# The indexer's low-part product over 128 rows, and two gate projections moved from the index loop to the threshold search

## The chip, the core and the metric

The kernel runs on one core of a Trainium2 chip. The core has a matrix engine (TensorE, PE in the profile), three engines for elementwise work (VectorE or DVE, ScalarE or ACT, GpSimd or POOL), and queues of transfers, here all issued by SyncE (SP). The engines run their own instruction lists in order and wait for one another at semaphores. The metric is the device time of one execution in microseconds; the time before is the median of three.

## What is computed

A trunk of two layers over 1024 tokens of 1024 channels, each with a mixer, a cross-attention of four heads into 256 memory tokens, a SiLU gate over all 2048 branch channels, an output projection and a layer norm. Layer A mixes by a depthwise convolution. Layer B, around which the change lies, is sparse attention: an indexer with 8 heads of 64 channels scores all keys for a query, the 256 best admissible keys are kept, and 12 attention heads work on those.

```python
iscore = relu(einsum('bqhd,bsd->bqhs', qib, k_idx))
iscore = einsum('bqh,bqhs->bqs', wb, iscore)
iscore = where(admiss, iscore, NEG)
_, sel = top_k(iscore, 256)
...                      # softmax attention over the selected keys, ALiBi distances
y = concatenate([y_mix, y_mem]) * silu(gate)
x = layer_norm(ALPHA * x + y @ w_out)
```

## The kernel before

All products run on TensorE in a float32 format of reduced width, so each operand is held as a high and a low part (`split_w`, `split_ps`), and a projection is three products per 128-row block: high by high (L149), high weight by low input (L151), low weight by high input (L153). `project_steps` gives them one at a time. A gate projection (`gate_steps`) is 128 gate columns for 1024 tokens: 2 halves of 512 columns, 8 blocks, 3 products, so 48 products of 512 columns, two silus on ScalarE (L706) and a store. Its weights come as two pieces of 256 KB through the SP queue (L122) into three raw buffers; ScalarE copies out the high part (L131), or GpSimd does (L129) where `pool_only` is set, and GpSimd subtracts for the low part (L132). High and low parts have six buffers, which is three gates.

The order in layer B is: projections for the indexer; the index loop; the threshold search and selection; attention.

The index loop goes over six query blocks (7, 6, 2, 5, 4, 3; block b has 128(b+1) keys) and in each over 8 index heads. Keys are cut into one or two parts of at most 512. For each part two products go into one PSUM bank. The stationary tile `t` has the 64 high-part channels of the head's queries in one half of its rows (`a`) and the 64 low-part channels in the other; `khh` holds the high part of the keys in both halves and `kll` their low part in both. So the first product (L777, all 128 rows) gives high times high plus low times high, and the second (L778, the 64 rows of `a`) adds high times low. ScalarE then takes the relu (L783; two PSUM tiles and two relu tiles) and VectorE multiplies by the head's weight and adds to the block's scores `xs` (L786, L788). After each head's last product, `FILL[b]` products of the first `FREE_GATES` gates are put into TensorE's list: 136 of 144 between the heads, and the rest behind the loop. There are 48 heads and 80 pairs of score products.

The threshold search finds the 256th largest score of each query bit by bit (31 rounds), with three blocks counted on VectorE (L829) and three on ScalarE (L835). The selection turns the scores into distances with a large one for what isn't selected (L896 to L905). Both have a low priority. The gates that are left, 12 of them, are put on TensorE behind the last score product, with `pool_only` weights, and after them the queries of the first two attention heads (`head_q`: 48 products each, and per half a copy on ScalarE, L806, and a subtraction on VectorE, L807). Attention scores (L951 to L953), their row maxima (L956) and the rest follow.

The order of instructions on each engine is made by a planner that simulates the engines, with the priorities above and `issue_after` edges; only what is quoted fixes a place by hand.

Of the kernel before, what the change touches and what calls it, by code (L numbers as in the profile page):

```python
# [18 lines left out]
PSUM = bass.MemoryType.PSUM  # L19

P = 128
T = 1024
# [31 lines left out]
FREE_GATES = 3  # L54
POOL_W = True
SELECT = (7, 4, 3, 6, 5, 2)
FILL = {7: 4, 6: 3, 5: 3, 4: 3, 3: 2, 2: 2}
# [7 lines left out]
def trunk(ctx, tc, x, mem, mem_g, mem_b, a_w_in, conv_w, conv_b, ln_g, ln_b,  # L65
          a_w_mkv, a_w_out, a_pg, a_pb, b_w_in, b_w_mkv, b_w_out, b_pg, b_pb, out, dbg=None):
    nc = tc.nc
# [13 lines left out]
    # ---------------------------------------------------------------- constants  # L81
# [7 lines left out]
    # per-channel vectors, channel on the partition: taps, conv bias, LN gain, LN bias, mem gain, mem bias  # L89
# [12 lines left out]
    # PSUM banks: projections ("pj") and the rest ("pt"), from the pools of the phase  # L102
# [14 lines left out]
    # ---------------------------------------------------------------- helpers  # L117
    def split_w(src3, shape, place=None, pool_only=False):
        """Loads a [128, 512]-word piece of a weight and splits it into two float32r parts."""
        n = uid()  # L120
        raw = wp.tile(shape, F32, tag="wraw", bufs=3, name=f"wr{n}")
        nc.sync.dma_start(raw, src3)  # L122
        if place is None:
            hi = wp.tile(shape, F32R, tag="whi", bufs=6, name=f"wh{n}")
            lo = wp.tile(shape, F32R, tag="wlo", bufs=6, name=f"wl{n}")
        else:
            hi, lo = place(n)
        if pool_only:
            nc.gpsimd.tensor_copy(hi, raw)  # L129
        else:  # L130
            nc.scalar.activation(hi, raw, AF.Copy)  # L131
        nc.gpsimd.tensor_tensor(lo, raw, hi.bitcast(F32), op=OP.subtract)  # L132
        return hi, lo

    def load_cols(w, c0, n=P, pool_only=False):
        """Columns c0:c0+n of a [1024, C] weight as two pieces of four 128-row blocks."""
        res = []
        for g in range(2):
            res.append(split_w(w[g * 512:(g + 1) * 512, c0:c0 + n].rearrange("(k p) c -> p k c", p=P), [P, 4, n],
                               pool_only=pool_only))  # L140
        return res

    def project_steps(pieces, mhi, mlo, c0, n, o):
        """o[cols, n] = W^T X over the moving operand's columns c0:c0+n, one product at a time."""
        for k in range(KD):
            hi, lo = pieces[k // 4]
            wh, wl = hi[:, k % 4, :], lo[:, k % 4, :]
            xh, xl = mhi[:, k, c0:c0 + n], mlo[:, k, c0:c0 + n]
            nc.tensor.matmul(o, wh, xh, start=(k == 0), stop=False)  # L149
            yield  # L150
            nc.tensor.matmul(o, wh, xl, start=False, stop=False)  # L151
            yield
            nc.tensor.matmul(o, wl, xh, start=False, stop=(k == KD - 1))  # L153
            yield

    def run(steps):
        """All that is left of some steps, and what they return."""
        while True:
            try:
                next(steps)  # L160
            except StopIteration as end:
                return end.value
# [12 lines left out]
    def ln_moments(src):  # L175
        """Mean and 1/sqrt(var + eps) of [128, 1024] along the free axis."""
        n = uid()
        st = small.tile([P, 2, 6], F32, tag="bnst", name=f"bnst{n}")
        for i in range(2):
            nc.vector.bn_stats(st[:, i, :], src[:, i * 512:(i + 1) * 512])  # L180
        mv = small.tile([P, 2], F32, tag="bnmv", name=f"bnmv{n}")
        nc.vector.bn_aggr(mv, st)
        rs = small.tile([P, 1], F32, tag="bnrs", name=f"bnrs{n}")
        nc.scalar.activation(rs, mv[:, 1:2], AF.Sqrt, bias=eps)
        nc.vector.reciprocal(rs, rs)
        return mv[:, 0:1], rs

    def ln_stats(src):
        """Scale and bias that normalize."""
        mean, rs = ln_moments(src)  # L190
        nb = small.tile([P, 1], F32, tag="bnnb", name=f"bnnb{uid()}")
        nc.vector.tensor_scalar(nb, mean, rs, -1.0, op0=OP.mult, op1=OP.mult)
        return rs, nb
# [7 lines left out]
    def layer_norm_late(dst, src, g, b, o):  # L201
        """The same in fewer steps, written out by halves."""
# [7 lines left out]
    def transpose_in(src, hi, lo, t, f=None):  # L210
        """[128 tok, 1024] -> columns t*128.. of the transposed hi and lo operands."""
# [11 lines left out]
    # ================================================================ layer A  # L223
    SC = {}
    with ExitStack() as actx:
# [14 lines left out]
        # ---- x and the vectors  # L240
# [29 lines left out]
        # ---- memory tokens: LN, transposed  # L270
# [23 lines left out]
        def mem_k(w, h, kv=None, raw=None):  # L294
            """K^T of one head of the memory attention, into kv = [K hi | V hi | K lo | V lo] or raw = [K | V]."""
# [8 lines left out]
        def mem_v(w, h, kv=None, raw=None):  # L304
            """V of one head, likewise."""
# [13 lines left out]
        def silu_gate(pl, w, c0, dst):  # L319
            """silu of 128 gate columns, transposed, into dst [128, 1024]."""  # L320
            pc = load_cols(w, c0)
            for hf in range(2):
                o = psum()
                project(pc, xhi, xlo, hf * 512, 512, o)
                nc.scalar.activation(dst[:, hf * 512:(hf + 1) * 512], o, AF.Silu)

        def mem_q(pl, tags, pc):
            """Queries of one head, transposed, in two parts; the products one at a time."""
# [9 lines left out]
        def mem_scores(pl, tags, q, kv, hf, banks_s):  # L338
            """Softmax over the memory tokens for half of the queries."""
# [26 lines left out]
        def mem_values(pl, tags, pn, kv, hf, sg, y, bank_pv, between=lambda ins: None):  # L366
            """Probabilities, transposed, times values, gated: half of y [128, 1024]."""
# [19 lines left out]
        # ---- gated conv input and the convolution  # L387
# [30 lines left out]
        def conv_pair(hs, i0):  # L418
            """Depthwise causal convolution of two channel tiles, taps interleaved."""
# [17 lines left out]
        def conv_stat(i):  # L437
            """Running sums over channels of the convolution less the mean of its first 128 channels."""
# [78 lines left out]
        # ---- conv LN statistics per token, then broadcast to all channels  # L517
# [22 lines left out]
        def load_y(pl, tag, src, dh, dl, gate=None, sub=None):  # L540
            """A branch in two parts, times silu(gate) where that is still to be done."""
# [23 lines left out]
        # ---- output projection of layer A  # L565
# [5 lines left out]
        def out_group(w_out, k0, yh, yl, acc, t_order, first=False, after=None, resident=None):  # L571
            """acc[tok, :] += y[:, 4 channel blocks] W_out[4 row blocks, :]."""
# [70 lines left out]
        def keep_a(hf, k):  # L643
            """Places for the last group's weights, all of which stay: four pieces where others are too."""
# [15 lines left out]
    # ================================================================ layer B  # L660
    with ExitStack() as bctx:
# [7 lines left out]
        def parts(b):  # L669
            """Key columns of a query block, cut into equal pieces of at most 512."""  # L670
# [28 lines left out]
        def gate_steps(pl, i, pool_only=False):  # L699
            """silu of 128 gate columns, transposed, into DRAM, one product at a time."""  # L700
# [10 lines left out]
        # ---- indexer  # L711
        with ExitStack() as ictx:
# [56 lines left out]
            for b in (7, 6, 2, 5, 4, 3):  # L769
# [3 lines left out]
                for h in range(IDX_HEADS):  # L773
                    t, a = qs[h]
                    S = psum_s()
                    for i, (c, m) in enumerate(pt):
                        nc.tensor.matmul(S[:, i, :m], t[:, blk], khh[:, c:c + m], start=True, stop=False)  # L777
                        step = nc.tensor.matmul(S[:, i, :m], t[a, blk], kll[a, c:c + m], start=False, stop=True)  # L778
# [18 lines left out]
        def head_q(h, pc):  # L797
            """Queries of a head, scaled by scale / slope; the products one at a time."""
# [11 lines left out]
        with ExitStack() as kctx:  # L810
            bm = kctx.enter_context(pool("bm"))

            # ---- exact 256th largest score of every query, bit by bit of its order-preserving key: state is the
            # float whose key has the bits found so far, and flipping a bit of it raises it (the lower bits of a
            # negative float count down). One group of blocks is counted on the vector engine (scores >= candidate),
            # the other on the scalar engine (scaled by 2^24, signs of candidate - score): there a candidate that is
            # itself a score may be refused, so the state may end one float low, which an exact count settles.
            def threshold():
# [44 lines left out]
                # scalar engine's group: drop what is too small to be a score, try the next float  # L863
# [13 lines left out]
            # ---- distances, with a large one where a key isn't selected (ties: lowest index first)  # L877
            def select():
# [7 lines left out]
                for b in SELECT:  # L886
# [12 lines left out]
                    # as many equal ones are taken as those above leave room for  # L899
# [20 lines left out]
        # ---- sparse attention: logits over slope in PSUM, one (head, two query blocks) step after the other  # L920
        with ExitStack() as tctx:
# [15 lines left out]
            def scores(h, j):  # L937
                """Softmax of query blocks 2j and 2j + 1."""
# [28 lines left out]
            def values(h, j, pt):  # L967
                """Transposed probabilities times values, gated."""
# [22 lines left out]
                for k in range(2 * j + 1):  # L991
                    nc.tensor.matmul(po, vh[:, k, :], ph[:, k, :], start=(k == 0), stop=False)
                    nc.tensor.matmul(po, vh[:, k, :], pl[:, k, :], start=False, stop=False)  # L993
                    if k == 2 * j:
                        # the last keys: for the second block only
# [40 lines left out]
            # one head after the other, scores a step ahead of values; between the products of a head run those of the  # L1036
            # next head's queries (of the last head: a gate that is left)
# [19 lines left out]
            def filler(i):  # L1057
                """Weights and steps of what runs beside head i of the sequence."""
# [19 lines left out]
            # places in the pool: what is written first lies clear of the selection's tiles  # L1078
# [22 lines left out]
    # ---- output projection of layer B  # L1101
# [66 lines left out]
```

## Time and profile before

| | us |
|---|---|
| median of 3 runs (lowest, highest) | 1740.03 (1739.72, 1742.56) |
| span of the profiled execution | 1739.0 |
| TensorE busy | 1677.7 |
| VectorE busy | 1171.7 |
| ScalarE busy | 756.5 |
| GpSimd busy | 688.5 |
| index loop, first to last of the main run of score products | 874.5 to 966.6 |
| threshold search and selection on VectorE | 968.2 to 1145.5 |

The profiled execution's own time is its span; no other time of it is listed, and the median of the runs is about one microsecond above it. A busy engine in this table is one that has an instruction in it. Products are pipelined, so the lengths of two that follow each other overlap, and what a product costs is the distance from its start to the next start.

### The profile page before, as it was taken

To read this page: it belongs to the slowest core of one execution; us is meant where nothing else is said; L and a number is where in the kernel's file an instruction comes from. 1 tells how busy PE (TensorE), PEld (TensorE's weight loads), DVE (VectorE), ACT (ScalarE), POOL (GpSimd) and SP (SyncE) were. 2 spreads that over 40 slices of the span, in tenths; PEclk is the share of its full clock that TensorE was granted. 3 is DMA by queue.
4 is the path that set the end of the run, shared out by engine and by line. 5 is a ranking of instruction groups with operands and counts; after the bars stand their busy time and mean duration, and the time that the engine had idled before them with its cause. 6 is when DMAs were issued, how large, how long until landed. Compare 5 with 4: busy or idle time off the path is not lost.

```text
span 1739.0 us, 22460 instructions
## 1 busy us (share of the span) xinstructions
PE 1677.7 (96%) x8214; PEld 1385.0 (80%) x8214; DVE 1171.7 (67%) x1800; ACT 756.5 (43%) x1416; POOL 688.5 (40%) x587
## 2 busy tenths in 40 slices
PE   7999999999999998999999999879999999999997
PEld 6877888888888876887855777668898988888886
DVE  3799999999995659256154899975545655535337
ACT  3333444443433514134453678455544544542121
POOL 2344554555546337334311333343223333343233
PEclk9999999999999998999999999989999999999999
DMA  5121222212233475122320233212112121137212
GB/s 180 49 61 61 85 61 73 82 63 90 69 110 122 146 278 169 61 80 88 93 56 25 74 91 90 75 37 80 62 55 73 61 80 49 61 120 266 93 43 97
DMA packets 138941, 156.88 MB, mean 90 GB/s; under 512 B 8074, under 2 KB 108426, under 8 KB 138832
## 3 DMA queue, kind: packets, MB, share of 16 engines
q1 hardware_dynamic: 138832, 155.47, 27.6%
q8 instruction: 64, 1.05, 0.2%
q14 instruction: 45, 0.37, 0.1%
HBM read 114.81 MB, written 38.80 MB: 88 GB/s over the span
## 4 chain that ended last, share of the span: by engine, by line
PE 62%; DVE 11%; ACT 3%; issue 2%; DMA 1%; POOL 1%; SPq 0%; DVEq 0%; ACTq 0%; POOLq 0%
PE pj L149 10%; PE pj L153 10%; PE pj L151 10%; PE pj L587 5%; PE pj L586 5%; PE pj L585 5%; DVE junk L829 3%; PE pt L981 2%; PE S L778 2%; PE S L951 1%; PE S L952 1%; PE S L953 1%; PE S L777 1%; PE pv L993 1%; PE pv L997 1%
## 5 line engine op out<-in xcount | busy, mean ns | idle before, releaser
L149 PE MATMUL pj<-xhi,wh 128*128 128x512 f32 (+2 forms) x1328 | 526.2, 396 | 17.6 <-DVE ql L807 3.6
L132 POOL TENSOR_TENSOR wl<-wr,wh 128x512 fp32r<-128x512 f32 (+1 forms) x260 | 350.8, 1355 | 460.6 <-ACT wh L131 444.9
L153 PE MATMUL pj<-xhi,wl 128*128 128x512 f32 (+2 forms) x1328 | 523.7, 394 | 0.0
L151 PE MATMUL pj<-xlo,wh 128*128 128x512 f32 (+2 forms) x1328 | 522.4, 393 | 0.6 <-DVE xlo L169 0.5
L433 DVE SCALAR_TENSOR_TENSOR acc<-h,chan,acc 128x996 f32<-128x996 f32 (+27 forms) x348 | 418.5, 1263 | 16.1 <-ACT acc L423 14.8
L149 PEld LDWEIGHTS pj<-xhi,wh 128*128 128x128 f32 (+1 forms) x1328 | 250.9, 189 | 73.8 <-DVE ql L807 6.9
L153 PEld LDWEIGHTS pj<-xhi,wl 128*128 128x128 f32 (+1 forms) x1328 | 250.9, 189 | 52.4 <-issue 3.7
L151 PEld LDWEIGHTS pj<-xlo,wh 128*128 128x128 f32 (+1 forms) x1328 | 251.1, 189 | 49.7 <-issue 2.0
L131 ACT ACTIVATE wh<-wr 128x512 fp32r<-128x512 f32 x236 | 147.2, 628 | 299.3 <-PE pj L151 155.4
L585 PE MATMUL pj<-wh,xhi 128*128 128x512 f32 x384 | 150.7, 399 | 9.3 <-DVE accA L592 5.6
L586 PE MATMUL pj<-wl,xhi 128*128 128x512 f32 x384 | 150.9, 395 | 0.0
L587 PE MATMUL pj<-wh,xlo 128*128 128x512 f32 x384 | 149.2, 394 | 0.0
L961 POOL TENSOR_SCALAR t<-t,smB 128x128 f32<-128x128 f32 (+3 forms) x96 | 71.6, 747 | 177.3 <-DVE smB L960 86.1
L956 DVE CUSTOM_DVE_ANT_0 t<-S,xs 128x128 f32<-128x128 f32 (+3 forms) x96 | 70.8, 755 | 64.9 <-PE S L953 42.9
L169 DVE TENSOR_TENSOR pl<-pt,ph 128x512 fp32r<-128x512 f32 (+1 forms) x120 | 69.2, 580 | 57.6 <-ACT ph L168 56.7
L585 PEld LDWEIGHTS pj<-wh,xhi 128*128 128x128 f32 x384 | 73.5, 191 | 27.6 <-DVE accA L592 6.4
L959 ACT ACTIVATE t<-t,mxB 128x128 f32<-128x128 f32 (+3 forms) x96 | 74.1, 774 | 49.0 <-DVE mxB L958 48.9
L168 ACT ACTIVATE ph<-pt 128x512 fp32r<-128x512 f32 (+1 forms) x120 | 60.2, 508 | 73.7 <-PE pt L981 67.7
L829 DVE TENSOR_SCALAR_CACHE_REDUCE junk<-xs,cand 128x1024 bf16<-128x1024 f32 (+2 forms) x93 | 89.9, 966 | 2.2
L835 ACT ACTIVATE junka<-xs,cand 128x896 bf16<-128x896 f32 (+2 forms) x93 | 80.3, 863 | 24.2 <-DVE cand L860 22.3
L587 PEld LDWEIGHTS pj<-wh,xlo 128*128 128x128 f32 x384 | 73.3, 191 | 16.0
L586 PEld LDWEIGHTS pj<-wl,xhi 128*128 128x128 f32 x384 | 73.4, 191 | 15.5
(273 smaller groups left out, 2726.4 us busy)
## 6 DMA issues: line engine op xcount, KB each, us to landing
wr<-in_a_w_in_dram SPq DMA_DIRECT2D x88, 256.0 KB
wr<-in_b_w_in_dram SPq DMA_DIRECT2D x76, 256.0 KB
wr<-in_a_w_out_dram SPq DMA_DIRECT2D x32, 256.0 KB
wr<-in_b_w_out_dram SPq DMA_DIRECT2D x32, 256.0 KB
yraw<-yb SPq DMA_DIRECT2D x16, 512.0 KB
gb<-gB SPq DMA_DIRECT2D x15, 512.0 KB
ga<-ga SPq DMA_DIRECT2D x12, 512.0 KB
gt<-ga SPq DMA_DIRECT2D x12, 512.0 KB
```

The lines of the kernel that those rows point to most:

```text
L131: nc.scalar.activation(hi, raw, AF.Copy)
L132: nc.gpsimd.tensor_tensor(lo, raw, hi.bitcast(F32), op=OP.subtract)
L149: nc.tensor.matmul(o, wh, xh, start=(k == 0), stop=False)
L151: nc.tensor.matmul(o, wh, xl, start=False, stop=False)
L153: nc.tensor.matmul(o, wl, xh, start=False, stop=(k == KD - 1))
L433: nc.vector.scalar_tensor_tensor(dst[:, s:], h[:, :T - s], w, acc[:, s:], op0=OP.mult, op1=OP.add)
L585: nc.tensor.matmul(o, yh[:, k, tsl], wh, start=(k == 0), stop=False)
L586: nc.tensor.matmul(o, yh[:, k, tsl], wl, start=False, stop=False)
L587: nc.tensor.matmul(o, yl[:, k, tsl], wh, start=False, stop=(k == 3))
L829: nc.vector.tensor_scalar(j[:, :nk(b)], xs(b), th[:, i:i + 1], None, op0=op, op1=OP.add, accum_out=c[:, i:i + 1])
L835: nc.scalar.activation(j[:, :nk(b)], xs(b), AF.Sign, bias=th[:, i:i + 1], scale=-(2.0 ** 24), accum_out=c[:, i:i + 1])
L959: nc.scalar.activation(t, t, AF.Exp, bias=mx[:, e:e + 1], scale=s, accum_out=sm[:, e:e + 1])
```

## The change

Two constants and one product change. In the index loop one gate product follows each head instead of two to four, and only gate 0 is computed there (48 heads, 48 products). Gates 1 and 2 go to the head of the list behind the loop, where their weights are split by GpSimd alone. The second score product takes all 128 rows of `t` and `kll`, so it adds low times low to high times low. The diff also removes comments and docstrings, which leaves the line numbers as they are.

```diff
-FREE_GATES = 3
+FREE_GATES = 1
-FILL = {7: 4, 6: 3, 5: 3, 4: 3, 3: 2, 2: 2}
+FILL = {7: 1, 6: 1, 5: 1, 4: 1, 3: 1, 2: 1}
...
                     for i, (c, m) in enumerate(pt):
                         nc.tensor.matmul(S[:, i, :m], t[:, blk], khh[:, c:c + m], start=True, stop=False)
-                        step = nc.tensor.matmul(S[:, i, :m], t[a, blk], kll[a, c:c + m], start=False, stop=True)
+                        step = nc.tensor.matmul(S[:, i, :m], t[:, blk], kll[:, c:c + m], start=False, stop=True)
```

## Rows read from the trace of the kernel before

**Rows 1.** The page: busy time of each engine, share of the span, instructions.

```profile
PE 1677.7 (96%) x8214; PEld 1385.0 (80%) x8214; DVE 1171.7 (67%) x1800; ACT 756.5 (43%) x1416; POOL 688.5 (40%) x587
```

**Rows 2.** Windows by engine: one stretch of the attention stage.

```profile
1300.00:1400.00 100.00, 98.97 (x607) 88.34 (x607) 54.95 (x155) 50.34 (x122) 33.11 (x41) 1.00 0.21 66
```

**Rows 3.** Timeline, TensorE: start, length, line, operands, idle before.

```profile
1145.80 0.69 PE L951 MATMUL S<-kh,qh 128*128 128x384 f32 x1 [10.13 <-DVE mxB L956]
```

**Rows 4.** Groups of instructions of the index loop, VectorE and ScalarE: count, busy, idle before.

```profile
L788 DVE SCALAR_TENSOR_TENSOR xs<-relu,win,xs 128x1024 f32<-128x1024 f32 (+5 forms) x42 | 43.0, 1025 | 37.6 <-ACT relu L783 37.4
L786 DVE TENSOR_SCALAR xs<-relu,win 128x1024 f32<-128x1024 f32 (+5 forms) x6 | 4.5, 750 | 6.2 <-ACT relu L783 6.2
L761 DVE TENSOR_TENSOR qs<-qw,hw 64x768 fp32r<-64x768 f32 x2 | 1.9, 952 | 0.8 <-ACT hw L756 0.8
...
L783 ACT ACTIVATE relu<-S 128x1024 f32<-128x1024 f32 (+5 forms) x48 | 36.4, 758 | 47.4 <-PE S L778 47.3
```

**Rows 5.** Timeline, TensorE, index loop: its begin, and a head of block 6.

```profile
874.51 0.40 PE L777 MATMUL S<-khh,qs 128*128 128x512 f32 x1
...
900.80 0.50 PE L153 MATMUL pj<-xhi,wl 128*128 128x512 f32 x1
...
901.90 0.47 PE L778 MATMUL S<-kll,qs 64*128 64x448 f32 x1
902.29 0.47 PE L777 MATMUL S<-khh,qs 128*128 128x448 f32 x1
902.69 0.46 PE L778 MATMUL S<-kll,qs 64*128 64x448 f32 x1
903.09 0.50 PE L153 MATMUL pj<-xhi,wl 128*128 128x512 f32 x1
```

**Rows 6.** Timeline, TensorE: gate products and attention scores, 128 rows each.

```profile
1009.79 0.39 PE L149 MATMUL pj<-xhi,wh 128*128 128x512 f32 x1
...
1029.96 0.39 PE L153 MATMUL pj<-xhi,wl 128*128 128x512 f32 x1
...
1151.53 0.37 PE L952 MATMUL S<-kl,qh 128*128 128x448 f32 x1
1151.74 0.36 PE L953 MATMUL S<-kh,ql 128*128 128x448 f32 x1
```

**Rows 7.** Line view of L777 and L778, weight loads: count, ns min/median/max.

```profile
L777 PEld LDWEIGHTS S<-khh,qs x80: 186/188/192, 865.2 to 965.6; 128*128 128x128 f32 x80
...
L778 PEld LDWEIGHTS S<-kll,qs x80: 182/183/183, 865.6 to 966.2; 64*128 64x128 f32 x80
```

**Rows 8.** Timeline, VectorE: ends of the index loop and of the selection.

```profile
876.50 0.75 DVE L786 TENSOR_SCALAR xs<-relu,win 128x1024 f32<-128x1024 f32 x1 [2.22 <-ACT relu L783]
879.12 1.28 DVE L788 SCALAR_TENSOR_TENSOR xs<-relu,win,xs 128x1024 f32<-128x1024 f32 x1 [1.87 <-ACT relu L783]
...
968.19 0.06 DVE L839 MEMSET z<- 128x6 f32 x1
...
1145.45 0.28 DVE L956 CUSTOM_DVE_ANT_0 t<-S,xs 128x128 f32<-128x128 f32 x1
```

**Rows 9.** Groups of instructions of the index loop, GpSimd.

```profile
L132 POOL TENSOR_TENSOR wl<-wr,wh 128x512 fp32r<-128x512 f32 x7 | 10.1, 1445 | 8.3 <-ACT wh L131 6.2 <-PE pj L153 2.0
L129 POOL CAST wh<-wr 128x512 fp32r<-128x512 f32 x5 | 3.0, 609 | 47.4 <-PE pj L151 26.8 <-issue 20.6
```

**Rows 10.** Groups of instructions of the threshold search, ScalarE: the gates' silus.

```profile
L706 ACT ACTIVATE gB<-pj 128x512 f32<-128x512 f32 x24 | 13.9, 580 | 4.0 <-PE pj L153 4.0
```

**Rows 11.** Windows by engine: the last stretches before attention, granted clock behind the engines.

```profile
1140.00:1145.00 5.00, 0.00 (x0) 0.00 (x0) 4.05 (x6) 1.81 (x2) 3.57 (x5) 0.50 0.39 128
1145.00:1150.00 5.00, 4.20 (x16) 3.82 (x17) 3.08 (x16) 2.33 (x8) 1.61 (x5) 0.55 0.41 134
```

**Rows 12.** Timeline, ScalarE and TensorE: the last gate's silu, a query product's wait.

```profile
1103.28 0.58 ACT L706 ACTIVATE gB<-pj 128x512 f32<-128x512 f32 x1
...
1117.88 0.50 PE L149 MATMUL pj<-xhi,wh 128*128 128x512 f32 x1 [3.64 <-DVE ql L807]
```

## The prediction

> **What bounds the kernel now.** I read the page's first part, then the windows by engine, then the groups of instructions of the index loop with what ended their idle time, then single instructions in order of time. TensorE is busy for 1677.7 of 1739.0 us [rows 1]; after the threshold stage it is busy for 98.97 of every 100 us [rows 2], so whatever moves the first attention product moves the end by as much. That product (L951, 384 columns) starts at 1145.80, after TensorE had stood idle for 10.13 us [rows 3]. So the place to work out is what lies before it: the index loop (L777 and L778 with gate products between them, from 874.5 to about 966.6) and the threshold search with the selection (VectorE, 968.2 to 1145.5).
>
> In the index loop the order of waits is: VectorE (L788) waits 37.4 us for ScalarE's relu, and ScalarE's relu (L783) waits 47.3 us for L778 [rows 4]. TensorE is the bound there, and it is slower than its columns: in one head of block 6 three gate products and four score products follow each other from 900.80 to 903.09, 2.29 us [rows 5]. Products of 128 rows elsewhere follow at 0.227 us for 512 columns (89 distances between the first two of these rows) and 0.21 us for 448 [rows 6]; three and four of them make 0.68 + 0.83 = 1.51 us. The rest, 0.78 us, stands at the two 64-row products: the reader is to see 0.40 us from start to start into and out of each L778, in place of 0.21. That is 0.39 us per 64-row product; the trace's 80 of them [rows 7] make about 31 us.
>
> After the loop the order turns over: the search is VectorE's own queue, TensorE fills the time with 12 gates, and then waits.
>
> **Index loop, widened product.** Nothing is added or removed but rows: 80 products of the same columns. I take the neighbours' spacing, since attention's low-part product L952, also a second product into the same bank, follows at it [rows 6]. Gain on TensorE 31 us; bounds 0 (the stall belongs to something else) and 32 us (0.40 a product, the stall read to the last hundredth of its seven starts).
>
> **Index loop, fewer gate products.** 136 products between the heads become 48; with the 8 left over that is 96 fewer, 96 x 0.227 = 21.8 us of TensorE, moved and not removed. TensorE's loop is then 160 score products of 422 columns on average (0.19 us, between the two spacings) = 30.5 us, plus 48 x 0.227 = 10.9: 41.4 us.
>
> **What is late next.** ScalarE's 48 relus take 36.4 us. VectorE has 43.0 (L788) + 4.5 (L786) + 1.9 (L761) = 49.4 us [rows 4]: it becomes the bound. Its first instruction of the loop starts at 876.50 and the next, 1.87 us idle, at 879.12, held by ScalarE's parts of the last query, which stay [rows 8]. So the loop ends at 876.5 + 1.9 + 49.4 = 927.8, say 928, instead of 968.2 where the search's first memset starts [rows 8]: 40 us earlier. Bounds: the three engines' shares are close and each has only two buffers, so handing over can cost 0.1 us a head (48 x 0.1 = 5 us, 933); if the 43.0 hold less GpSimd interference than before, 2 us earlier (926). GpSimd's share: the weights of the next gates are now all split there (0.61 us cast, L129, and 1.4 us subtraction, L132); 5 casts and 7 subtractions stand in the old loop [rows 9], and as six buffers hold three gates' pieces, about as many come in the shorter one. The 43.0 us contain their price once, so I add nothing.
>
> **Beside the search and the selection.** VectorE's queue from its first memset (968.19) to the row maximum (L956, 1145.45) is 177.3 us [rows 8]. The 24 silus that fall into the search on ScalarE are set by the pace of gate products (24 x 0.227 = 5.4 us each), and that pace is the same: still about 24 within the search. The moved gates' four silus (0.58 us [rows 10]) come beside the selection, where ScalarE is less than half busy [rows 11]: nothing there; up to 4 x 0.58 = 2.3 us if each stands ahead of a relu that VectorE's next step needs. Their weights' DMAs (four of 256 KB, on SP) and their four extra casts (4 x 0.61 = 2.4 us on GpSimd) go ahead of the query weights in the same queues; GpSimd has room, yet casts that fall beside VectorE can hold it: 0 to 3 us. I take 2 us for both. VectorE's queue then reaches the row maximum at 928 + 177.3 + 2 = 1107.
>
> TensorE from the last score product (about 2.5 us before VectorE's end): the old 12 gates and 8 products, 584, ran from 966.6 to the last silu at 1103.28 [rows 12], 136.7 us or 0.234 each. 14 gates are 672 x 0.234 = 157 us, so 925.5 + 157 = 1082.5. Then 96 query products: 21.8 us unhindered (1104.3), or the 32.4 us that they took, from 1103.3 to 1135.67 (1145.80 less 10.13), because their banks wait for two instructions (L806, L807) in queues full of the selection (3.64 us before L149 [rows 12]): 1114.9. So TensorE and VectorE meet there, where TensorE had ten idle microseconds. I take 1108 for the first product: it is nearest to VectorE's queue, since the query products now lie wholly inside the selection. That is 37.8 us earlier.
>
> [...]
>
> **Sum.** 37.8 + 1 = 38.8 us off the profiled span of 1739.0: 1700.2. The median of the runs lies 1.0 us above that span: 1701. Gates 1 and 2 fill idle TensorE time (10.13 us and the stalls of the query products); without that cover they would cost up to 21.8 us.
>
> **Rivals.**
> (a) TensorE ends last in front of attention: the query products take 32.4 us again, the first product comes at 1115, 31 us earlier, with 0 to 1 us of clock: 1709. For it: both meet within 3 us. Against: ScalarE and VectorE have those instructions in the order of a plan that is made anew.
> (b) The rows don't matter: L778's weights load in 183 ns against 188 for L777's 128 rows [rows 7], so the load itself is no shorter or longer, and if the stall came from the change of moving operand it would stay. The loop is then 41.4 + 31 = 72 us of TensorE, ending near 949: 19 us earlier; TensorE then needs 157 + 21.8 to 32.4 us: 1125 to 1136, 10 to 20 us earlier: 1725. Against: L951 to L953 and L149 to L153 change operands too and don't stall [rows 6]. [...]
> (c) The slower one: with one gate product per head TensorE waits a little in each head (1.03 us of work against 1.15 of VectorE's in block 6), and the clock falls to its lower level for the loop. Each of the 208 products doubles: 83 us, the loop ends at about 960, TensorE's 157 + 32.4 us end at 1147, the first product is 1 to 2 us later than now, on a clock that falls again: 1742. It decides from the point where the granted clock stays under 0.6 for nearly the whole loop; for half of it the result is 1720. For it: the clock fell to 0.5 after the idle at 1140. Against: that idle was ten microseconds, these are tenths of one; and in the low state TensorE would be busy without a break. [...]
>
> **Numbers.** Forecast (VectorE paces both stretches, 1694 to 1706) 0.70; (a) 0.17; (b) 0.05; (c) 0.08, of which 0.03 is slower than now. The range reaches from 1691 (loop ending at 926, no loss in the selection, clock back, and TensorE's floor) to 1716, which takes in (a) and a hand-over cost of 5 us beside it, and leaves out (b) and (c). About 0.2% (3.5 us) is what a measurement of this kernel can tell from no change. Faster 0.95, same 0.02, slower 0.03.
>
> **What would show it.** Right: L777 and L778 spaced alike, at 0.21 us for 448 columns; the relu's wait for L778 mostly gone and VectorE near 90% busy in a loop of about 50 us; search's first memset near 928; the first 384-column L951 near 1108 with TensorE idle before it for under 6 us; attention unchanged at 99%. Wrong: 0.40 us spacing left at L778 (b), a clock under 1.00 in the loop (c), the query products as the last thing ahead of L951 (a), or a loop longer than 57 us with none of these, which would mean that the hand-over of buffers between the three engines is the bound and I mis-sized it.

## The result, and the profile after

The changed kernel runs in 1714.09 us (median, 1713.22 to 1715.64), against 1739.88 us: a ratio of 0.9856 with a 95% interval of 0.9845 to 0.9868, 25.8 us less. A later set of runs of it (the control below) gave 0.9869, 0.9854 to 0.9883. Its profiled span is 1713.6 us, 25.4 below the old one.

The page's busy times of the changed kernel:

```profile
PE 1651.4 (96%) x8214; PEld 1381.1 (81%) x8214; DVE 1173.3 (68%) x1800; ACT 753.3 (44%) x1412; POOL 694.7 (41%) x591
```

TensorE's busy time fell by 26.3 us against [rows 1], about as much as the span, and the attention stage is as full as it was (98.97 of the 100 us from 1300 to 1400, as in [rows 2]). The loss and gain lie before it.

**The index loop.** The timeline of TensorE in a head of block 6, as in [rows 5]:

```profile
885.33 0.47 PE L777 MATMUL S<-khh,qs 128*128 128x448 f32 x1
885.63 0.37 PE L778 MATMUL S<-kll,qs 128*128 128x448 f32 x1
885.84 0.37 PE L777 MATMUL S<-khh,qs 128*128 128x448 f32 x1
886.04 0.37 PE L778 MATMUL S<-kll,qs 128*128 128x448 f32 x1
886.25 0.39 PE L153 MATMUL pj<-xhi,wl 128*128 128x512 f32 x1
886.72 0.47 PE L777 MATMUL S<-khh,qs 128*128 128x448 f32 x1
```

All four score products now have 128 rows. The first opens the head after a wait, and the second starts 0.30 us behind it; from there on they follow at 0.20 to 0.21 us in place of 0.40, and the gate product too. The head takes 1.39 us with one gate product, where the old one took 2.29 with three. The groups of the loop, answering to [rows 4]:

```profile
L788 DVE SCALAR_TENSOR_TENSOR xs<-relu,win,xs 128x1024 f32<-128x1024 f32 (+5 forms) x42 | 42.2, 1004 | 8.8 <-ACT relu L783 5.3
...
L783 ACT ACTIVATE relu<-S 128x1024 f32<-128x1024 f32 (+5 forms) x48 | 35.7, 758 | 14.9 <-DVE xs L788 12.7 <-PE S L778 1.9
```

ScalarE's relu waited 47.3 us for L778 before; 1.9 us of that are left, and it now waits 12.7 us for VectorE to give a relu buffer back. VectorE itself waits 5.3 us instead of 37.4. The bound has moved from TensorE to the two elementwise engines. VectorE's timeline, at the places of [rows 8]:

```profile
874.29 0.80 DVE L786 TENSOR_SCALAR xs<-relu,win 128x1024 f32<-128x1024 f32 x1 [3.51 <-ACT relu L783]
...
930.42 0.06 DVE L839 MEMSET z<- 128x6 f32 x1
...
1105.74 0.56 DVE L905 SCALAR_TENSOR_TENSOR xs<-xs,dist 128x384 f32<-128x384 f32 x1 [0.95 <-POOL dist L904]
...
1113.56 0.29 DVE L956 CUSTOM_DVE_ANT_0 t<-S,xs 128x128 f32<-128x128 f32 x1 [4.22 <-PE S L953]
```

The loop's first instruction starts at 874.29 and the search's memset at 930.42: 56.1 us in place of 91.7. The selection ends at 1106.3, but the row maximum that followed it at once before (1145.45, [rows 8]) now comes at 1113.56: between them VectorE has only two query subtractions (L807, 0.7 us each) to do, and waits at the end for score products.

**In front of attention.** TensorE's waits from 930 to 1120 (line, what it waited for: us in total, times, longest), and TensorE's and ScalarE's timelines there:

```profile
PE pj L149 <- ACT gB L706: 10.8, 6, 4.3
```

```profile
1100.34 0.50 PE L149 MATMUL pj<-xhi,wh 128*128 128x512 f32 x1 [4.33 <-ACT gB L706]
...
1119.19 0.34 PE L951 MATMUL S<-kh,qh 128*128 128x384 f32 x1
```

```profile
1098.44 0.84 ACT L903 ACTIVATE eq<-eq 128x768 f32<-128x768 f32 x1 [5.06 <-DVE eq L902]
...
1099.70 0.58 ACT L706 ACTIVATE gB<-pj 128x512 f32<-128x512 f32 x1
...
1104.45 0.58 ACT L806 ACTIVATE qh<-pj 128x512 fp32r<-128x512 f32 x1
```

The first 384-column L951 starts at 1119.19, not after a wait but straight behind the last query products and two score products: TensorE ends last. (It is not the first product of attention, as the prediction calls it. In both kernels six score products of 256 columns stand among the query products before it, here from 1107.53; but it is the place where the old kernel's idle stood.) It had waited 10.8 us for silus. The reader is to see the longest of these waits on ScalarE: the last gate's silu starts at 1099.70, because it stands in ScalarE's list behind a relu of the selection (L903) that had to wait for VectorE until 1098.44; the product that needs the bank starts at 1100.34. The first query copy (L806, 1104.45) stands behind the selection's last relu. Windows of the changed kernel (us, then busy of PE, PEld, DVE, ACT and POOL, then the clock):

```profile
874.00:931.00 57.00, 50.93 (x217) 35.97 (x216) 47.62 (x54) 39.56 (x54) 9.79 (x19) 1.00 0.12 32
1080.00:1090.00 10.00, 7.47 (x27) 5.65 (x26) 9.96 (x14) 3.16 (x5) 2.72 (x4) 0.83 0.36 105
...
1100.00:1110.00 10.00, 9.66 (x36) 7.82 (x37) 6.58 (x9) 3.43 (x7) 7.08 (x8) 0.83 0.63 207
```

In the loop the clock stayed at 1.00; in front of attention, beside the idle (TensorE busy for 7.47 and 9.66 of 10 us), it was 0.83 over 1080 to 1090 and over 1100 to 1110.

### The profile page after: what moved, and what is told of

Read it like the earlier page. It is cut to its first block, busy times and chain, and to the rows that moved or that the text cites. A ratio compares the mean times of both kernels' runs of the same rounds, so it can differ in the third digit from the quotient of the medians.

```text
span 1713.6 us, 22459 instructions
## 1 busy us (share of the span) xinstructions
PE 1651.4 (96%) x8214; PEld 1381.1 (81%) x8214; DVE 1173.3 (68%) x1800; ACT 753.3 (44%) x1412; POOL 694.7 (41%) x591
## 4 chain that ended last, share of the span: by engine, by line
PE 57%; DVE 14%; ACT 4%; issue 3%; DMA 2%; POOL 1%; SPq 0%; DVEq 0%; ACTq 0%; POOLq 0%
PE pj L149 9%; PE pj L151 9%; PE pj L153 9%; PE pj L587 5%; PE pj L585 5%; PE pj L586 5%; DVE junk L829 4%; PE pt L981 2%; DVE xs L788 2%; PE S L951 1%; ACT junka L835 1%; PE S L953 1%; PE S L952 1%; PE pv L993 1%; PE pv L997 1%
## 5 line engine op out<-in xcount | busy, mean ns | idle before, releaser
L149 PE MATMUL pj<-xhi,wh 128*128 128x512 f32 (+2 forms) x1328 | 523.9, 395 | 19.1 <-ACT gB L706 10.8
L132 POOL TENSOR_TENSOR wl<-wr,wh 128x512 fp32r<-128x512 f32 (+1 forms) x260 | 352.5, 1362 | 433.7 <-ACT wh L131 412.6
L585 PE MATMUL pj<-wh,xhi 128*128 128x512 f32 x384 | 149.2, 395 | 11.2 <-DVE accA L592 7.7
L961 POOL TENSOR_SCALAR t<-t,smB 128x128 f32<-128x128 f32 (+3 forms) x96 | 71.6, 747 | 183.1 <-DVE smB L960 87.5
L956 DVE CUSTOM_DVE_ANT_0 t<-S,xs 128x128 f32<-128x128 f32 (+3 forms) x96 | 70.9, 756 | 72.7 <-PE S L953 49.8
L959 ACT ACTIVATE t<-t,mxB 128x128 f32<-128x128 f32 (+3 forms) x96 | 74.1, 774 | 46.3 <-DVE mxB L958 46.0
```

The costliest lines, as they stand in the source:

```text
L585: nc.tensor.matmul(o, yh[:, k, tsl], wh, start=(k == 0), stop=False)
L959: nc.scalar.activation(t, t, AF.Exp, bias=mx[:, e:e + 1], scale=s, accum_out=sm[:, e:e + 1])
```

## The experiments

The theory after the result: the 128 rows take away TensorE's stall and shorten the loop by more than the whole gain; the two moved gates then make TensorE the last before attention, and lose part of it again. Rivals: the gain comes from moving gates into idle time; TensorE's end is set by its banks, or by where silus and query copies stand in ScalarE's list.

**The rows alone** (e1).

```diff
 # against the changed kernel
-FREE_GATES = 1
+FREE_GATES = 3
-FILL = {7: 1, 6: 1, 5: 1, 4: 1, 3: 1, 2: 1}
+FILL = {7: 4, 6: 3, 5: 3, 4: 3, 3: 2, 2: 2}
```

> The widened product alone: three gates between the score products as before, 128 rows for L778. Theory (rows remove the stall, and the changed kernel's loss lies in the moved gates' silus, which stand behind the selection's steps in ScalarE's list while TensorE waits for their two banks): TensorE's loop is 30.5 + 136 x 0.227 = 61.4 us, spacing at L778 0.21 us for 448 columns, the search's first memset near 938 (before 968.2), TensorE's wait for silus before attention under 3 us, time about 1709 (1706 to 1713), so as fast as the changed kernel or faster. Rival (the gain comes mainly from moving gates into idle time): the time stays above 1725.

1708.97 us, 0.9829 (0.9812 to 0.9845). VectorE's and TensorE's timelines:

```profile
938.54 0.06 DVE L839 MEMSET z<- 128x6 f32 x1
...
1115.37 0.69 PE L951 MATMUL S<-kh,qh 128*128 128x384 f32 x1 [10.41 <-DVE mxB L956]
```

The search starts at 938.5 and attention's L951 at 1115.37, after 10.41 us of idle, as in the old kernel; the whole stage has moved forward by 30 us. As expected, to the microsecond. One edited line gives the whole gain and more.

**The move alone** (e2).

```diff
-nc.tensor.matmul(S[:, i, :m], t[:, blk], kll[:, c:c + m], start=False, stop=True)
+nc.tensor.matmul(S[:, i, :m], t[a, blk], kll[a, c:c + m], start=False, stop=True)
```

> The two gates moved alone: one gate between the score products, 64 rows for L778 as before. Theory (rows remove the stall): spacing at L778 stays at 0.40 us, TensorE's loop is 30.5 + 31 + 10.9 = 72 us and TensorE-bound, the search starts near 949 instead of 930, everything after it as in the changed kernel: about 1733 (1729 to 1738). Rival (rows don't matter, fewer products between the heads made the gain): about 1714.

1742.1 us (1729.99 to 1745.94), 1.0011 (0.9989 to 1.0032): no gain at all, and 9 us worse than expected. TensorE's timeline in block 6, then its windows:

```profile
889.26 0.46 PE L778 MATMUL S<-kll,qs 64*128 64x448 f32 x1
889.65 0.50 PE L153 MATMUL pj<-xhi,wl 128*128 128x512 f32 x1
889.99 0.36 PE L777 MATMUL S<-khh,qs 128*128 128x448 f32 x1
890.28 0.46 PE L778 MATMUL S<-kll,qs 64*128 64x448 f32 x1
890.67 0.47 PE L777 MATMUL S<-khh,qs 128*128 128x448 f32 x1
```

```profile
904.00:914.00 10.00, 10.00 (x32) 5.13 (x31) 5.90 (x10) 6.20 (x11) 0.50 (x2) 1.00 0.00 0
...
924.00:934.00 10.00, 10.00 (x27) 5.16 (x27) 4.66 (x7) 4.33 (x6) 2.66 (x3) 0.81 0.01 2
934.00:944.00 10.00, 10.00 (x19) 4.85 (x18) 3.73 (x5) 2.71 (x4) 0.14 (x1) 0.50 0.10 26
```

The spacing behind L778 is still 0.39 us, so the rows are what removes it. But the clock, which I had left out of this expectation, fell: from about 930 it was 0.50, although TensorE had an instruction in it for every microsecond of these stretches (10.00 of 10). The search started at 958.8 instead of 949. Two of the ten runs kept a mean clock of 0.99 and took 1730 us, as expected; the others had 0.98 and took 1740 to 1746. With 64-row products, then, the clock was 1.00 all through the old loop (874 to 967), with two to four gate products per head, and 0.50 at the end of this one, with one, in the profiled execution. The parts don't add: alone they give 30 us and nothing, together 26.

**Both score products on 64 rows** (e5), for the cause of the stall. Low times high and low times low are left out.

```diff
-nc.tensor.matmul(S[:, i, :m], t[:, blk], khh[:, c:c + m], start=True, stop=False)
-step = nc.tensor.matmul(S[:, i, :m], t[:, blk], kll[:, c:c + m], start=False, stop=True)
+nc.tensor.matmul(S[:, i, :m], t[a, blk], khh[a, c:c + m], start=True, stop=False)
+step = nc.tensor.matmul(S[:, i, :m], t[a, blk], kll[a, c:c + m], start=False, stop=True)
```

> As the changed kernel, but both score products take the 64 rows of a (low times high and low times low are left out, so the scores differ a little). Theory (the change of row count between neighbouring products costs, not the 64 rows): within a head L777 to L778 and L778 to L777 follow at 0.21 us for 448 columns, and 0.40 us is left only into and out of the gate product. Rival (a 64-row product itself is slow): 0.40 us everywhere. The time says little: 1715 to 1740.

One run, 1754.47 us. TensorE's timeline in block 7 (512 columns), while the clock was still 1.00, and two windows:

```profile
880.19 0.50 PE L151 MATMUL pj<-xlo,wh 128*128 128x512 f32 x1
880.62 0.50 PE L777 MATMUL S<-khh,qs 64*128 64x512 f32 x1
880.96 0.40 PE L778 MATMUL S<-kll,qs 64*128 64x512 f32 x1
881.20 0.39 PE L777 MATMUL S<-khh,qs 64*128 64x512 f32 x1
881.43 0.39 PE L778 MATMUL S<-kll,qs 64*128 64x512 f32 x1
881.75 0.49 PE L153 MATMUL pj<-xhi,wl 128*128 128x512 f32 x1
```

```profile
874.00:884.00 10.00, 9.59 (x31) 5.10 (x30) 8.09 (x7) 7.69 (x9) 2.12 (x2) 1.00 0.37 93
...
894.00:904.00 10.00, 10.00 (x21) 5.76 (x20) 4.61 (x4) 3.62 (x5) 0.00 (x0) 0.50 0.00 0
```

From 64 rows to 64 rows the products come down to 0.23 and 0.24 us, as 128-row products of 512 columns do (0.227). The rest stands around the changes of row count: 0.43 us from the gate product to the first score product and 0.34 to the next, 0.32 from the last one to the gate product. The five products take 1.56 us where five at 0.227 take 1.14: 0.42 us for two changes, 0.21 each, and the old kernel's 0.78 us in a head ([rows 5]) had four changes, 0.20 each. So here 64 rows are not slow, changing the row count is. The time is worse than my expectation's end (1740), because the clock was at 0.50 from about 885 to 970.

**One gate moved instead of two** (e3).

```diff
-FREE_GATES = 1
+FREE_GATES = 2
-FILL = {7: 1, 6: 1, 5: 1, 4: 1, 3: 1, 2: 1}
+FILL = {7: 2, 6: 2, 5: 2, 4: 2, 3: 2, 2: 2}
```

> As the changed kernel, but two gates between the score products (two products behind each head) and one moved. Theory: TensorE's loop is 30.5 + 96 x 0.227 = 52.3 us beside VectorE's 50 or so, so the search starts within 3 us of the changed kernel's 930.4, while 11 us of gate products are gone from behind it: the last silus come before most of the selection, TensorE's waits for silus fall from 10.8 to under 7 us, time 1706 (1702 to 1711). Rival (what ends last is the two queries' copies at the end of the selection, whatever the gates do): 1714 within 2 us.

1707.69 us, 0.9823 (0.9808 to 0.9837), clear of the changed kernel's interval. VectorE's and TensorE's timelines:

```profile
930.41 0.06 DVE L839 MEMSET z<- 128x6 f32 x1
...
1107.59 0.56 DVE L905 SCALAR_TENSOR_TENSOR xs<-xs,dist 128x384 f32<-128x384 f32 x1 [1.81 <-POOL dist L904]
```

```profile
1109.54 0.34 PE L951 MATMUL S<-kh,qh 128*128 128x384 f32 x1
```

The loop still ends at 930.4, though it began 1.3 us earlier (872.97): 48 more gate products in it cost about 1 us. The selection's end (1108.2) and the first 384-column L951 (1109.54) now lie 1.4 us apart. Waits for silus are 6.3 us, as expected.

**No gate in the loop** (e8).

```diff
-FREE_GATES = 1
+FREE_GATES = 0
-FILL = {7: 1, 6: 1, 5: 1, 4: 1, 3: 1, 2: 1}
+FILL = {7: 0, 6: 0, 5: 0, 4: 0, 3: 0, 2: 0}
```

> As the changed kernel, but no gate at all between the score products, all 15 behind them. Theory: VectorE still paces the loop, the granted clock stays at 1.00 in it with 128-row products, the search's first memset stays within 2 us of 930, and the 48 further products add their 11 us before attention: 1724 (1720 to 1730). Rival (gate products are what holds the clock up in the loop): the clock falls to the lower level, the loop is longer than 60 us and the time above 1735.

1722.05 us, 0.9903 (0.9888 to 0.9918). TensorE's windows in the loop:

```profile
884.00:894.00 10.00, 8.95 (x33) 6.37 (x32) 8.73 (x8) 7.15 (x8) 0.62 (x1) 0.87 0.01 2
894.00:904.00 10.00, 8.29 (x31) 5.60 (x31) 8.11 (x12) 6.48 (x12) 0.50 (x2) 0.83 0.00 0
904.00:914.00 10.00, 8.32 (x40) 5.85 (x39) 8.84 (x10) 7.36 (x10) 0.49 (x1) 1.00 0.00 1
```

The search started at 925.5, 5 us earlier than expected: the loop began 1.8 us earlier and took 53.0 us in place of 56.1. The clock sagged to 0.83 and was 1.00 again from 904. The first 384-column L951 came at 1126.66. With e3 this makes a scale. From the last score product (927.75 in e3, 926.91 in the changed kernel, 923.18 here) to that L951, 13, 14 and 15 gates behind the loop take 181.8, 192.3 and 203.5 us, that is 10.5 and 11.2 us more for each 48 products of 0.227 us (10.9 us). So behind the loop the amount of TensorE's work sets the time: with 13 gates its end meets VectorE's, and from 14 on it ends last.

**Four banks** (e4) for gate halves instead of two.

```diff
-                o = psum()
+                o = psum_t() if hf else psum()
```

> As the changed kernel, but the second half of every gate takes its bank from the other pair (pt), so four banks instead of two take gate products. Theory (TensorE waits because only two banks hold halves whose silus are queued behind the selection on ScalarE): TensorE's wait for silus falls from 10.8 to under 3 us, the first 384-column L951 comes near 1110 instead of 1120, time 1704 (1702 to 1709). Rival (the place of the silus and of the query copies in ScalarE's and VectorE's lists is the bound, banks or not): 1714 within 2 us.

1716.37 us, 0.9873 (0.9858 to 0.9888): the rival's side. TensorE's waits (870 to 1160):

```profile
PE S L951 <- ACT qh L806: 9.9, 1, 9.9
...
PE pj L149 <- ACT gB L706: 3.4, 1, 3.4
PE pj L149 <- DVE ql L807: 1.1, 1, 1.1
```

The waits for silus fell to 3.4 us as the theory said, and 9.9 us came back at once in front of attention's first L951, for the first head's query copy. The banks were not the bound.

**Queries before the last two gates** (e6), and the same with one gate moved (e7).

```diff
-                for i in gates[FREE_GATES:]:
+                for i in gates[FREE_GATES:-2]:
                     for _ in gate_steps(bm, i, POOL_W):
                         pass
-            for h in range(EARLY_Q):
-                run(head_q(h, load_cols(b_w_in, h * P)))
+                for h in range(EARLY_Q):
+                    run(head_q(h, load_cols(b_w_in, h * P)))
+                for i in gates[-2:]:
+                    for _ in gate_steps(bm, i, POOL_W):
+                        pass
```

> As the changed kernel, but the queries of the first two heads stand before the last two gates in TensorE's list instead of behind them. Theory (what ends last is the first head's queries, whose copies on ScalarE and VectorE come behind the selection's last steps because gates stand before them): the first query copies come during the selection, the row maximum follows VectorE's selection within 2 us of 1107, the first 384-column L951 comes near 1110, time 1704 (1700 to 1710). Rival (whatever stands last before attention waits as long, gates or queries): 1714 within 2 us.

> Two gates between the score products, one moved, and the queries before the last two gates. Theory: both gains together, bounded by VectorE's selection: the first 384-column L951 near 1108, time 1702 (1698 to 1707). Rival: once one gate stays in the loop, VectorE's selection ends last already, and the order adds nothing: 1708 within 2 us.

e6: 1718.79 us, 0.9887 (0.987 to 0.9904), against my theory. TensorE's waits (870 to 1160; its line numbers are three higher from here on, so L954 is L951 and L959 is L956):

```profile
PE pj L149 <- DVE ql L807: 6.3, 3, 3.8
...
PE S L954 <- DVE mxB L959: 4.4, 1, 4.4
PE pj L149 <- ACT gB L706: 2.5, 4, 1.3
```

Now the gates stand last, and they wait as the queries did, 6.3 us for query subtractions. But VectorE's row maximum waited too, and longer (waits of VectorE, 1100 to 1130):

```profile
DVE t L959 <- DMA gb<-gB: 17.0, 1, 17.0
```

The profile puts that wait down to the store of the last gate's silus, and by it L954 started at 1125.68, 4.4 us after TensorE was ready. So this edit brought a wait of its own, and its time does not measure the order alone. Without that wait L954 could have started at 1121.3, still no earlier than in the changed kernel. e7: 1707.22 us, 0.9817 (0.9799 to 0.9836), no different from e3, as its rival said.

**The selection's relu off ScalarE**: on GpSimd (e9, and e10 with one gate moved), and on VectorE (e12); e11 is the changed kernel as control.

```diff
-                    nc.scalar.activation(eq, eq, AF.Relu, scale=BIG)
+                    nc.gpsimd.tensor_scalar(eq, eq, BIG, 0.0, op0=OP.mult, op1=OP.max)   # e9, e10
+                    nc.vector.tensor_scalar(eq, eq, BIG, 0.0, op0=OP.mult, op1=OP.max)   # e12
```

> As the changed kernel, but the selection's relu (L903), which on ScalarE stands ahead of the last gates' silus and the query copies and waits there for VectorE, runs on GpSimd in front of L904. Theory (the silus' place behind instructions that wait for VectorE is what stops TensorE before attention): TensorE's waits for silus fall from 10.8 to under 4 us, the first 384-column L951 comes near 1111, time 1706 (1702 to 1710). Rival (TensorE has 768 products to do behind the loop and ends last anyway): 1712 or more. [...]

> Two gates between the score products, one moved, and the selection's relu on GpSimd. Theory: with one gate kept in the loop VectorE's own queue (loop, search, selection) ends last within a few us of TensorE, so freeing ScalarE gives little: 1706 (1703 to 1709), against 1708 without. Rival (silus wait here too and cost all of their 6 us): 1702.

> The changed kernel itself, as the control for the two others on the same chip: 1714 (1712 to 1717).

> As the changed kernel, but the selection's relu (L903) runs on VectorE, between the L902 before it and the steps behind it: no wait for VectorE is left at it on ScalarE, and no 3 us instructions on GpSimd as in the try before. VectorE's queue grows by six instructions of 0.4 to 0.8 us, about 3.5 us, to 1110. Theory (the silus' place stops TensorE): waits for silus under 5 us in place of 10.8, the first 384-column L951 near 1113, time 1708 (1704 to 1711). Rival (the 768 products behind the loop end last however the silus stand): 1714 or more.

e9 took 1721.02 us (0.99, 0.9883 to 0.9916), e10 1721.78 (0.9898, 0.9883 to 0.9912), e11 1716.04. GpSimd needed up to 4.23 us for what ScalarE does in 1.06, and the selection ended over 14 us later (1120.9 in e9): the two say nothing on the question. e12 does: 1716.02 us, 0.9874 (0.9857 to 0.989), the control's time. TensorE's waits in it:

```profile
PE pj L149 <- ACT gB L706: 4.7, 4, 3.0
PE pj L149 <- DVE ql L807: 3.7, 1, 3.7
PE S L951 <- ACT qh L806: 3.6, 1, 3.6
```

The waits for silus went from 10.8 to 4.7 us, and 7.3 us stood up again at the query copies, which were in ScalarE's list behind L895 this time. In e4, e6 and e12 I took away or moved one wait, and each time about as much appeared at another instruction of the same chain: up to that L951 TensorE waited 14.4, 10.3 and 12.0 us in all, against 10.8. So this part of my theory fell: no single place of a silu costs the time. TensorE has some 174 us of products behind the loop and waits 10 to 15 us in all for copies that share lists with the selection; both together are more than VectorE's 177 us. Whether another order of all of them would bring the waits down is open.

## Why the prediction was right, and where its size was off

The time lies in the range (1691 to 1716), near its end, and the sign was right; the forecast time was 13 us too low.

**The widened product** was right in mechanism and size: 0.20 us spacing, and 30 us alone (e1) against 31 worked out. Rival (b) is excluded by e2 and e5. L778's load takes 187 to 192 ns (median 189) with 128 rows and took 182 to 183 (median 183) with 64 ([rows 7]): 6 ns more, so the load is not where the 0.39 us of a 64-row product stood. What a change of row count costs is some 0.21 us (e5); why it costs that, no run shows.

**What is late next** was right: VectorE paces the loop. Its length was 56.1 us against 51.3 worked out. VectorE was busy for 47.6 us of it, where I had 49.4, and idle for 8.5, where I had 1.9. The difference of the idle, 6.6 us, is the hand-over between engines that I had put at up to 5 us and left out of the sum; the profile puts 5.3 of the 8.5 down to ScalarE's relu, and the rest are short gaps between instructions. TensorE's timeline shows 1.39 us for a head of block 6, where VectorE's L788 takes 1.15. As the loop began 2.2 us earlier, it ended at 930.4 against 928. The GpSimd interference that I had bounded at 2 us stands in the old loop's timeline: an L788 of 896 columns takes 1.15 us there, but 1.82 beside a subtraction of GpSimd's (899.57, L132 at 899.16) and 1.52 beside a cast (906.43, L129 at 906.40). L788's busy time went from 43.0 to 42.2 us.

**VectorE's queue to the selection's end** was right: 1106.3 against 1107.

**The term that was mis-sized** is the last: "I take 1108 for the first product: it is nearest to VectorE's queue, since the query products now lie wholly inside the selection." It was 1119.19, which is 11.2 of the 13.4 us by which the span missed; rival (a), to which I gave 0.17, is what happened. From the last score product (926.9) to 1119.19 TensorE took 192.3 us: 768 products at 0.227 us are 174.3, waits for silus 10.8, and the clock of 0.83 in two stretches of 10 us takes up to 3.4 by my estimate (0.17 of 20 us); the other 3.8 us I can't place. What I had at nothing is TensorE's waits: I had the query products once with them (32.4 us, 1114.9) and once without (21.8 us, 1104.3), and let the first go because the query products would lie inside the selection. They ended over 12 us behind it. The old kernel's TensorE took 169.5 us from its last score product (966.2) to its last query product (1135.7), 15.1 us more than 680 products at 0.227, and 7.9 us of that were waits. The changed kernel has 88 products more, 20.0 us, and 18.0 us beside its products: two more gates stood on top of a loss that stayed, only that its waits are now at the silus, which I had costed as ScalarE time (0 to 2.3 us). The ten idle microseconds of the old kernel were room for one gate (e3), not for two.

**Clock.** Right for the loop: it stayed at 1.00 with one 128-row gate product per head, so rival (c) did not come, although TensorE was busy for only 6.96 of the 10 us from 874 to 884. The clock can fall in this loop nevertheless: with 64 rows (e2, e5) it went to 0.50. In e2 that was not by (c)'s small waits, since TensorE was busy for 10.00 of 10 us in every stretch from 874 to 934. And the argument against (c), that TensorE "would be busy without a break" in the low state, did not hold as a reason: from 934 to 954 it was, 10.00 of 10 us, and the clock stayed at 0.50. The changed kernel's TensorE stood idle for 6.1 of the 57 us from 874 to 931, at a clock of 1.00. What brought the clock down in e2 stays open.

No run shows the 1 us that the sum adds for the clock. In front of the first 384-column L951 the clock was 1.00 (1110 to 1120) where it had been 0.50 ([rows 11]), and the product is 0.34 us long (0.69 in [rows 3]), but from it to the end the span is 594.4 us, and it was 593.2. With the 1 us these are the other 2.2 us of the miss; why the stage is 1.2 us longer is not explained.

## What to carry to other kernels

Look at start-to-start distances of neighbouring products wherever a stationary operand changes its number of rows: filling the rows, even with terms that don't matter, was worth 30 us here and one line. Moving work into an engine's idle time pays only up to the idle that is there, and waits that stood in that stretch before are not to be counted as room; here one gate of 48 products was free and the second cost 6 us, and the place to stop was where the two engines' ends meet (1108.2 and 1109.5). When work that sits between other products is taken out, the granted clock is the first thing to look at: in the loop it went from 1.00 to 0.50 with 64-row products (e2), and to 0.83 with 128-row products and no gate between them (e8).

The version with one gate moved (e3) is the one to keep: 1707.7 us, against 1714.1 for the change and 1709.0 for the rows alone, of which the last is not told apart from it.

## What the runs showed that I had not expected

TensorE can be shown busy for 10.00 of 10 us and still be granted a clock of 0.50 (e2 from 934 to 959, e5 from 894 to 964). In e2 it was shown busy all the time before the clock fell, too (10.00 of 10 from 874 on); in e5 it stood idle for 0.9 us of the 20 before 894. The changed kernel's TensorE, on 128-row products, stood idle for 3.0 us of 10 in its loop and kept 1.00:

```profile
874.00:884.00 10.00, 6.96 (x29) 4.62 (x27) 7.61 (x7) 7.58 (x9) 2.23 (x2) 1.00 0.37 93
```

And GpSimd's price seems to hang on the operation: in e9 multiply and maximum on 1024 columns took 4.23 us, while the two multiplies of L961 on 1024 columns take 1.13 us in the same kernel's attention stage. At 384 columns it is 1.50 us against 0.59. How much of this is waiting and not work, no run here separates:

```profile
L903 POOL TENSOR_SCALAR eq<-eq 128x1024 f32<-128x1024 f32 x1 | 4.2, 4229 | 7.6 <-DVE eq L902 7.6
...
L961 POOL TENSOR_SCALAR t<-t,smB 128x1024 f32<-128x1024 f32 x6 | 6.8, 1126 | 2.8 <-DVE smB L960 2.5
```
